# Three sums of weight blocks on GpSimd instead of VectorE, and a new order of the head, in a matmul-tanh-multiply kernel

## The chip, the cores and the metric

The kernel runs on one core of a Trainium2 chip. The metric is the device time of one execution in microseconds, the median of several runs. The engines are named as in the profile: PE (TensorE), DVE (VectorE), ACT (ScalarE), POOL (GpSimd) and SP (SyncE, which only issues DMAs here).

## The reference

```python
x  = randn(16, 512, 1024)   # float32
w1 = randn(1024, 768)
w2 = randn(1024, 768)

def reference(x, w1, w2):
    y1 = np.matmul(x, w1)
    y2 = np.matmul(x, w2)
    return (np.tanh(y1) * y2).astype(np.float32)
```

## The kernel before

The 8192 rows of x are 64 row tiles of 128 ("x rows" below, x0 to x63). Each needs two products with 1024 x 768 weights. The kernel stores w1 and w2 as f16 in one tile `wh`, in rows k0 to k7 of 128 input channels; `u` is w1 and `v` is w2, so u3 is row k3 of w1. It multiplies with f16 on PE and sums in PSUM.

The first four x rows (the head) are done plainly: for each, the chains a (w1, columns 0 to 511), b (w2, the same columns) and G (the last 256 columns of both), of 8 matmuls of 512 columns each (`mm`, L522). The b chain of x3 is kept for the end. The other 60 x rows are done in 20 triples, each with a scheme of fewer multiplications than plain blocks need: 15 block products instead of 18. Each product (`product`, L550) is four matmuls of 512 columns and multiplies a sum of x blocks (`x_sum`, L507, tile `s`) with a sum of w blocks (`w_sum`, L497, tile `b`). The sums are numbered as bit masks: for w, bits 0, 1, 2 are the blocks a, b, G of k0 to k3 and bits 3, 4, 5 those of k4 to k7. So b24 = block 8 + block 16 needs u4 to u7 and v4 to v7; b26 = block 2 - b24; b45 = b37 - block 8. Eleven sums of w blocks, 128 x 2048 f16 each, are made once, on DVE (`B_SUMS`), and then used in all 20 triples. The products that use the three sums above are p1 (s3 with b24), p12 (s35 with b26) and p4 (s10 with b45); b24 also goes into b29 and this into b27, which p0 uses. Ten sums of x blocks are made for each triple (`A_SUMS`), on DVE too, which besides adds partial results (`c_add`, L560) and multiplies with tanh (L529 in the head, L567 in the triples). ACT does tanh, copies out of PSUM and half of the casts of loaded f32 rows to f16 (L427; DVE's casts are L429).

The rows u, v and x0 to x3 are loaded as f32 by the queues of SP and ACT in the order of `SP_LOADS` and `ACT_LOADS` (`y` is an x row). x rows from x4 on are loaded by POOL's queue, in f16 (`load_x`, L471); the first of them (x4 to x6) are transposed on PE like the head's (L463), the later ones by DMA from SP's queue (L474). POOL does no other work but small copies of one column (`gate_x`, L586), which make a load wait until an earlier transpose has landed.

The order of the instructions on each engine is made while the program is built: `Planner.run` gives every operation a duration, a due time and the operations that it needs, and places them. The due times of the head's matmuls are set by `PE_HEAD` (an entry `1a0` is the first half of the a chain of x1, an entry `p7` a product of the first triple) and `HEAD_START`, those of others backwards from their users with `MARGIN`. On the chip there is no clock: each engine takes its instructions in this order, and each waits for the semaphores of what it needs. While data is late PE multiplies constants (`WARM`, and `FILLERS` at named places; L857).

Of the kernel before, what the change touches and what calls it, by code (L numbers as in the profile page):

```python
# [75 lines left out]

PE_HEAD = ("1a0 0a1 1b1 0b1 1G1 p7 p1 0a0 3a0 2b1 p6 0G0 2a1 1b0 1G0 3a1 "
           "p10 3G1 0b0 p9 p12 2G1 p8 1a1 p11 p14 2b0 0G1 3G0 2G0 2a0")  # L80
HEAD_START = 2.5

PE_LAST = "p10 p7 p6 p13- p0- p12 p9 p11 p4- p5- p8 p0 p1 p3- p4 p5 p13 p2- p3 p14 p2 h0 h1"
MUL_DUE = 0.022
MARGIN = {"S": 0.407, "B": 0.262, "T": 5.87, "L": 9.71, "early": 0.060}


WARM = (512, 512, 256)  # L90
FILLERS = {"PT1.0": (512,), "m1b2": (192,), "m1b7": (256,), "PT2.1": (448,)}

EARLY_LOADS = {0: 0.2}
SP_LOADS = ("y0 y1 v7 u3 y2 u1 v4 u0 v0 "
            "v1 v3 u2 u4 v5 v6 u6 u5 u7")
ACT_LOADS = "y3 v2"
POOL_LOADS = "5.0:v5 4.0 4.1 5.1 6"  # L100


class Planner:
# [15 lines left out]
    def op(self, name, engines, due, needs, fn, *args, behind=(), issued=(), chains=(), dma=None, seeds=False, slack=0.0, soon=None):  # L119

        assert name not in self.ops, name
        self.ops[name] = dict(engines=engines, due=due, needs=[n for n in needs if n], behind=[n for n in behind if n],
                              issued=[n for n in issued if n], fn=fn, args=args, chains=chains, dma=dma, seeds=seeds, slack=slack, soon=soon)
        for c in chains:
            self.chains.setdefault(c, {"left": 0, "bank": None})["left"] += 1
# [197 lines left out]
    def spare(self, n):  # L325

        t = self.start_of[n]
        return [b for b in range(len(self.held)) if all(t <= a or z <= t - 1.0 for a, z in self.held[b])][0]


@with_exitstack
def kernel(
# [9 lines left out]
    B, M, K = x.shape  # L342
# [4 lines left out]
    F = 512  # L347
# [9 lines left out]
    PACE, STORES, ST_HEAD, ST3G = "4544", (1.56, 2.37, 3.04), (12, 17, 19), 100  # L357
    sp_loads = ["L" + n for n in SP_LOADS.split()]
    act_loads = ["L" + n for n in ACT_LOADS.split()]
    XF_BUFS, XG_BUFS = 3, max((SP_LOADS + ACT_LOADS).count("y"), 1)  # L360
    ISSUE_SP, ISSUE_ACT, TABLE = 0.495, 0.52, 1.28
# [9 lines left out]
    pool = lambda name, bufs, **k: fast.enter_context(tc.tile_pool(name=name, bufs=bufs, **k))  # L371
# [6 lines left out]
    banks = [pspool.tile([P, F], f32, name=f"bank{i}") for i in range(8)]  # L378
# [24 lines left out]
    plan = Planner(8)  # L403
    op = plan.op
# [189 lines left out]
    DVE_F, DVE_G, DVE_S, DVE_B, DVE_W = (0.60, 0.69), (0.33, 0.42), (0.34, 0.42), (1.23, 1.27), (0.47, 0.56)  # L594
# [3 lines left out]

    head = PE_HEAD.split()
    head_at = {entry: HEAD_START + n * SLOT for n, entry in enumerate(head)}  # L600
    ORIGIN = HEAD_START + (len(head) - 15) * SLOT
    sequence, slot_of = [], {}
# [15 lines left out]
    at, held_at = END - len(tail) * SLOT, {}  # L618
# [8 lines left out]
    parts, early, last, back = {}, set(), "", []  # L627
    both = sorted([(ISSUE_ACT * z, "act", z, n) for z, n in enumerate(act_loads)] + [(ISSUE_SP * z, "sp", z, n) for z, n in enumerate(sp_loads)])
    issuer, last_on = {}, {"act": "", "sp": ""}
    for _, e, z, n in both:  # L630
# [14 lines left out]
        elif n[1] == "x":  # L645
            z = n[2:]
# [19 lines left out]
    last, xh_order, on_pe = "", [], {}  # L666
    for entry in POOL_LOADS.split():
        z, _, gated = entry.partition(":")
        mt, h = (int(v) for v in (z + ".-1").split(".")[:2])
        lo, n = (0, KO) if h < 0 else (h * KH, KH)  # L670
# [29 lines left out]
    for c in "aGb":  # L700
        for mt in range(HEAD):
# [9 lines left out]
            xt_readers[mt] += last  # L711
            due = max(head_at[f"{mt}{c}{h}"] for h in range(2)) + MUL_DUE
            if c == "a":
# [10 lines left out]
    def casts(v):  # L724
        bit = v.bit_length() - 1
        ks = range(bit // 3 * KH, (bit // 3 + 1) * KH)
        return [f"c{c}{k}" for c in ("u", "v", "uv")[bit % 3] for k in ks]

    def w_needs(v):
        return [f"B{v}"] if v in wsum else casts(v)  # L730

    for v, a, b, how in B_SUMS:
        op(f"B{v}", {"dve": DVE_B}, None, w_needs(a) + w_needs(b), w_sum, v, a, b, how)

    def x_needs(i, v):
        if v & (v - 1):
# [24 lines left out]
    for i in range(TRIPLES):  # L761
        until = {}
# [3 lines left out]
    for i in range(TRIPLES):  # L766
# [6 lines left out]
        for o in C_OPS:  # L773
# [19 lines left out]
            if kind in ("t", "th"):  # L793
                lo, n = (0, F) if kind == "t" else (F, G)
                op(f"{name}.{i}", {"act": ACT_F if n == F else ACT_G}, due, needs, c_tanh, i, r, o[4], lo, n, o[5],
                   behind=reuse_out(mt), chains=chains)
            else:
                lo, n, at = (0, F, 0) if kind == "m" else (F, G, G)
# [50 lines left out]

    plan.backward(lambda n: MARGIN["early"] if n in early else MARGIN.get(n[0], 0.2))  # L850
    order = plan.run()
# [3 lines left out]
    def constants(b, n):  # L855

        pin(nc.tensor.matmul(b[:, :n], ones, ones[:, :1].to_broadcast([P, n]), start=True, stop=True))  # L857

    for z, n in enumerate(WARM):
        constants(banks[z], n)  # L860
    first = sp_loads[:2]
# [4 lines left out]
    for n in order:  # L866
        if n not in first:
            o = plan.ops[n]
            for z in FILLERS.get(n, ()):
                constants(banks[plan.spare(n)], z)  # L870
            o["fn"](plan.engine_of[n], *o["args"])
    fast.close()

# [106 lines left out]
```

## Time and profile before

| | |
|---|---|
| median of 3 runs | 298.87 us (298.63 to 299.97) |
| span of the profiled execution | 297.3 us |
| DMA | 64.55 MB, mean 217 GB/s |
| PE clock granted | full in all slices |

A profile row names the source line, the engine, the operation, the tiles written and read, and the shapes. In the rows in order of time the first two numbers are the start and the length in us, counted from the start of the span; "xN" merges N equal instructions that follow each other, and the brackets give the idle time before and what ended it. In the rows of groups the numbers behind the bar are busy us and the mean ns of one instruction. In the chain of waits each row is a piece of the chain that ended last.

### The profile page before, as it was taken

Reading aid. Unit: us, or ns where it says so; the run is one execution under the profiler, and the core shown is the slowest. Engines: PE = TensorE matmul, PEld = TensorE weight load, DVE = VectorE, ACT = ScalarE, POOL = GpSimd, SP = SyncE. Lnnn points to the kernel's source line nnn. Section 1 sums busy time; section 2 is a strip of 40 time slices with the busy share of each in tenths; the row PEclk is TensorE's granted clock in tenths of the full one; section 3 lists DMA queues with packets and bytes.
Section 4 is the critical chain, followed back from the end, with each engine's and each line's share of the span. In section 5 each row is a group of like instructions: output and inputs, shape, how many; then the busy total and the mean of one; then the engine's idle time right before and its main releaser. Section 6 shows DMA issues by size and latency. Waiting matters only on the chain.

```text
span 297.3 us, 4698 instructions
## 1 busy us (share of the span) xinstructions
PE 290.9 (98%) x1419; PEld 137.7 (46%) x1419; DVE 255.5 (86%) x517; ACT 227.6 (77%) x450; POOL 46.7 (16%) x122
## 2 busy tenths in 40 slices
PE   6999999999999999999999999999999999999995
PEld 3545444444444675444444444444444444444443
DVE  1458999999988999898899988989899898999685
ACT  3798988996969769697876979788696866867561
POOL 1024040211030111113121010212101030000000
PEclk9999999999999999999999999999999999999999
DMA  7999999999999999999999999999989899681316
GB/s 263 406 403 230 162 169 222 242 251 258 110 317 212 221 255 244 221 215 259 161 227 217 172 223 199 246 224 215 226 169 245 164 279 244 144 240 47 119 55 215
DMA packets 82827, 64.55 MB, mean 217 GB/s; under 512 B 62704, under 2 KB 64752, under 8 KB 82800
## 3 DMA queue, kind: packets, MB, share of 16 engines
q1 hardware_dynamic: 73584, 47.59, 62.6%
q0 software_dynamic: 8928, 15.73, 34.3%
q10 hardware_dynamic: 288, 0.92, 0.8%
q8 instruction: 11, 0.18, 0.3%
q14 instruction: 16, 0.13, 0.1%
HBM read 39.85 MB, written 25.17 MB: 219 GB/s over the span
## 4 chain that ended last, share of the span: by engine, by line
PE 91%; DMA 6%; ACT 1%; SPq 0%; DVE 0%; issue 0%
PE bank L550 87%; DMA w_f<-in_w_dram 4%; PE bank L522 3%; DMA x_f<-in_x_dram 2%; ACT wh L427 1%; PE bank L463 1%; SPq L423 0%; DVE o_last L529 0%; SPq L415 0%; PE bank L580 0%
## 5 line engine op out<-in xcount | busy, mean ns | idle before, releaser
L550 PE MATMUL bank<-b,s 128*128 128x512 f16 (+1 forms) x664 | 148.1, 371 | 0.0
L550 PEld LDWEIGHTS <-s 128*128 128x128 f16 x832 | 81.2, 98 | 91.4 <-DVE s L507 0.6
L553 ACT ACTIVATE s<-bank 128x512 f32<-128x512 f32 x100 | 58.6, 595 | 41.0 <-PE bank L550 40.5
L560 DVE TENSOR_TENSOR bank<-bank,s 128x512 f32<-128x512 f32 x100 | 69.5, 697 | 18.1 <-PE bank L550 7.8
L477 ACT ACTIVATE junk<-xh 128x1024 f16<-128x1024 f16 x64 | 67.3, 1051 | 0.2
L567 DVE TENSOR_TENSOR o<-o,bank 128x512 f32<-128x512 f32 (+1 forms) x120 | 63.1, 548 | 2.5 <-ACT o L563 1.7
L550 PEld LDWEIGHTS <-xT 128*128 128x128 f16 x412 | 40.3, 98 | 46.1 <-ACT xT L427 0.2
L550 PE MATMUL bank<-b,xT 128*128 128x512 f16 (+1 forms) x252 | 58.5, 369 | 0.0
L563 ACT ACTIVATE o<-bank 128x256 f32<-128x256 f32 (+1 forms) x80 | 33.0, 432 | 12.4 <-PE bank L550 6.1
L550 PE MATMUL bank<-wh,s 128*128 128x512 f16 (+1 forms) x168 | 41.1, 369 | 0.0
L550 PE MATMUL bank<-wh,xT 128*128 128x512 f16 x160 | 40.9, 379 | 0.0
L586 POOL COPY held_x<-xT 128x1 f16<-128x1 f16 x52 | 12.2, 235 | 165.1 <-DMA xT<-xh 165.0
L471 POOL DMA_DIRECT2D xh<-in_x_dram x62 | 33.3, 540 | 20.3 <-issue 6.6
L507 DVE TENSOR_TENSOR s<-s,xT 128x512 f16<-128x512 f16 x80 | 32.3, 421 | 1.2
L563 ACT ACTIVATE o<-s 128x512 f32<-128x512 f32 x40 | 24.9, 623 | 1.2 <-DVE s L560 1.2
L507 DVE TENSOR_TENSOR s<-xT 128x512 f16<-128x512 f16 x60 | 25.0, 418 | 0.0
L553 ACT ACTIVATE bank<-bank 128x512 f32<-128x512 f32 x40 | 21.7, 573 | 1.6 <-DVE bank L560 0.9
L522 PE MATMUL bank<-wh,xT 128*128 128x512 f16 x72 | 18.8, 378 | 0.3
L507 DVE TENSOR_TENSOR s<-xT,s 128x512 f16<-128x512 f16 x40 | 16.7, 417 | 0.0
L560 DVE TENSOR_TENSOR bank<-s,bank 128x512 f32<-128x512 f32 x20 | 13.9, 694 | 1.6
L560 DVE TENSOR_TENSOR s<-s,bank 128x512 f32<-128x512 f32 x20 | 13.6, 681 | 0.3 <-ACT s L553 0.3
L477 ACT ACTIVATE junk<-wh 128x768 f16<-128x768 f16 x16 | 13.5, 842 | 0.2
(42 smaller groups left out, 120.6 us busy)
## 6 DMA issues: line engine op xcount, KB each, us to landing
out_dram<-o SPq DMA_DIRECT2D x54, 384.0 KB, 4.7
xh<-in_x_dram POOLq DMA_DIRECT2D x58, 256.0 KB, 5.7
w_f<-in_w_dram SPq DMA_DIRECT2D x15, 384.0 KB, 6.3
out_dram<-o SPq DMA_DIRECT2D x9, 256.0 KB, 2.0
x_f<-in_x_dram SPq DMA_DIRECT2D x3, 512.0 KB, 4.7
out_dram<-o SPq DMA_DIRECT2D x9, 128.0 KB, 1.7
xT<-xh SPq DMA_TRANSPOSE x57, 5.3
x_f<-in_x_dram ACTq DMA_DIRECT2D x1, 512.0 KB, 4.9
```

Of the source, the lines that this page charges most:

```text
L427: pin(nc.scalar.copy(dst, src))
L463: pin(nc.tensor.transpose(b[:, (k - lo) * P:(k - lo + 1) * P], xhs[mt][:, k * P:(k + 1) * P], ident_h))
L471: pin(nc.gpsimd.dma_start(xhs[mt][:, lo * P:(lo + n) * P], xf[mt][:, lo * P:(lo + n) * P]))
L477: pin(nc.scalar.activation(junk[:, :src.shape[-1]], src, ACT.Abs, scale=scale, accum_out=sums[:, column:column + 1]))
L507: pin(engine[e].tensor_tensor(ss[i, v], x_operand(i, a), x_operand(i, b), OP[how]))
L522: pin(nc.tensor.matmul(shaped(bank(chain)[:, lo:lo + n], w), xts[mt][:, k, :], w, start=begun[chain] == 1, stop=begun[chain] == KO, skip_g ...
L550: pin(nc.tensor.matmul(to, x_operand(i, a)[:, k, :], w, start=begins and k == 0, stop=k == KH - 1, skip_group_check=True))
L553: pin(nc.scalar.activation(place(i, dst, True), place(i, src), ACT.Copy, scale=float(sign)))
L560: pin(nc.vector.tensor_tensor(d, a, b, ALU.add if signs == (1, 1) else ALU.subtract))
L563: pin(nc.scalar.activation(out_tile(HEAD + 3 * i + r)[:, lo:lo + n], place(i, src)[:, :n], ACT.Tanh, scale=float(sign)))
L567: pin(nc.vector.tensor_tensor(o, o, place(i, src)[:, at:at + n], ALU.mult))
L586: pin(nc.gpsimd.tensor_copy(held_x, xts[mt][:, 0, :1]))
```

## The change

Three of the eleven sums of w blocks, b26, b45 and b24, are made on POOL (`POOL_B`). All the tables that set the order of the head are replaced: `PE_HEAD`, `HEAD_START`, `MUL_DUE`, `MARGIN`, the orders of loads for the three queues, and the list of fillers, which is now worked out from the planner's own gaps (`fillers`).

```diff
-PE_HEAD = ("1a0 0a1 1b1 0b1 1G1 p7 p1 0a0 3a0 2b1 p6 0G0 2a1 1b0 1G0 3a1 "
-           "p10 3G1 0b0 p9 p12 2G1 p8 1a1 p11 p14 2b0 0G1 3G0 2G0 2a0")
-HEAD_START = 2.5
+PE_HEAD = ("0a1 0b1 p1 3a0 2a1 1a0 3G1 1G1 3G0 0G1 1a1 0G0 p7 p6 2b1 p10 p9 0a0 1b0 p12 1G0 0b0 2G1 "
+           "2b0 3a1 p8 p11 p14 2a0 1b1 2G0")
+HEAD_START = 4.535
-MUL_DUE = 0.022
-MARGIN = {"S": 0.407, "B": 0.262, "T": 5.87, "L": 9.71, "early": 0.060}
+MUL_DUE = -1.445
+MARGIN = {"S": 0.773, "B": 0.02, "T": 3.425, "L": 8.221, "early": 0.01}
-FILLERS = {"PT1.0": (512,), "m1b2": (192,), "m1b7": (256,), "PT2.1": (448,)}
-SP_LOADS = ("y0 y1 v7 u3 y2 u1 v4 u0 v0 "
-            "v1 v3 u2 u4 v5 v6 u6 u5 u7")
-ACT_LOADS = "y3 v2"
-POOL_LOADS = "5.0:v5 4.0 4.1 5.1 6"
+SP_LOADS = "y0 v4 y1 u3 u4 v0 u1 v7 v1 u2 v3 v5 u6 u7 u5 v6"
+ACT_LOADS = "y2 y3 u0 v2"
+POOL_B = (26, 45, 24)
+POOL_LOADS = "5.0:v5 6 5.1 4.0 4.1"
...
+    def fillers(self, until):
+
+        found, busy = {}, None
+        for n in sorted((n for n in self.ops if self.engine_of[n] == "pe"), key=lambda n: self.start_of[n]):
+            t = self.start_of[n]
+            if t > until:
+                break
+            if busy is not None and t - busy > 0.32 and self.spare(n):
+                found[n] = self.spare(n)[0], int((t - busy - 0.12) * 600) // 32 * 32
+            busy = t + self.ops[n]["engines"]["pe"][0]
+        return found
...
-        op(f"B{v}", {"dve": DVE_B}, None, w_needs(a) + w_needs(b), w_sum, v, a, b, how)
+        op(f"B{v}", {"pool": (4.6, 4.7)} if v in POOL_B else {"dve": DVE_B}, None, w_needs(a) + w_needs(b), w_sum, v, a, b, how)
...
+    fillers = plan.fillers(24.0)
...
-            for z in FILLERS.get(n, ()):
-                constants(banks[plan.spare(n)], z)
+            if n in fillers:
+                b, z = fillers[n]
+                for at in range(0, z, F):
+                    constants(banks[b], min(F, z - at))
```

What this does to the order of the built program is seen at three places. The source lines of the change are 11 higher (w_sum is L508, x_sum L518, load_x L482), 14 at the end.

On POOL, behind the copy that starts the x loads (`held`). `xh` with a number is an x row; before, the sums are not there:

```order
L589 COPY held_88<-w_f_227 128x1
L471 DMA xh_277<-in_x_dram 128x512
L471 DMA xh_282<-in_x_dram 128x512 x2
L471 DMA xh_277<-in_x_dram 128x512
L471 DMA xh_296<-in_x_dram 128x1024
L471 DMA xh_301<-in_x_dram 128x1024
L471 DMA xh_305<-in_x_dram 128x1024
L471 DMA xh_312<-in_x_dram 128x1024
L471 DMA xh_318<-in_x_dram 128x1024
L471 DMA xh_425<-in_x_dram 128x1024
```

And with the change:

```order
L482 DMA xh_300<-in_x_dram 128x1024
L482 DMA xh_304<-in_x_dram 128x1024
L482 DMA xh_311<-in_x_dram 128x1024
L508 TENSOR_TENSOR b24_101<-wh_95 128x2048
L482 DMA xh_383<-in_x_dram 128x1024
L508 TENSOR_TENSOR b26_106<-wh_95,b24_101 128x2048
L482 DMA xh_447<-in_x_dram 128x1024
L508 TENSOR_TENSOR b45_102<-b37_100,wh_95 128x2048
L597 COPY held_x_89<-xT_404 128x1
L482 DMA xh_497<-in_x_dram 128x1024
```

The sums stand between the loads of x9 to x12, which wait for them on POOL's queue.

On DVE, from the cast of the last w row that DVE casts (`w_f_256` is u7, in the change `w_f_258` is v6) to the first sums of x. Before:

```order
L429 CAST wh_95<-w_f_256 128x768
L497 TENSOR_TENSOR b24_101<-wh_95 128x2048
L497 TENSOR_TENSOR b36_98<-wh_95 128x2048
L529 TENSOR_TENSOR o_333<-o_333,bank7_84 128x512
L497 TENSOR_TENSOR b37_100<-wh_95,b36_98 128x2048
L507 TENSOR_TENSOR s3_379<-xT_341 128x512
L507 TENSOR_TENSOR s10_382<-xT_341,xT_366 128x512
L507 TENSOR_TENSOR s11_390<-s3_379,xT_366 128x512
L507 TENSOR_TENSOR s15_394<-s11_390,xT_366 128x512
```

With the change:

```order
L440 CAST wh_95<-w_f_258 128x768
L508 TENSOR_TENSOR b36_98<-wh_95 128x2048
L540 TENSOR_TENSOR o_last_323<-o_last_323,bank2_79 128x256
L508 TENSOR_TENSOR b37_100<-wh_95,b36_98 128x2048
L540 TENSOR_TENSOR o_326<-o_326,bank4_81 128x512
L540 TENSOR_TENSOR o_331<-o_331,bank5_82 128x512
L440 COPY xT_369<-bank4_81 128x512
L440 COPY xT_355<-bank2_79 128x512
L508 TENSOR_TENSOR b18_103<-wh_95 128x2048
L518 TENSOR_TENSOR s3_399<-xT_369 128x512
L540 TENSOR_TENSOR o_326<-o_326,bank3_80 128x256
L518 TENSOR_TENSOR s11_411<-s3_399,xT_355 128x512
```

b24 is gone from this place; two products and two copies out of PSUM (banks) and the sum b18 stand ahead of s3, the sum that the first product p1 reads.

On SP, the loads at the start (`x_f` is an x row in f32, `w_f` a row of w). Before:

```order
L415 DMA x_f_120<-in_x_dram 128x1024
L415 DMA x_f_122<-in_x_dram 128x1024
L423 DMA w_f_133<-in_w2_dram 128x768
L423 DMA w_f_135<-in_w1_dram 128x768
L415 DMA x_f_137<-in_x_dram 128x1024
L423 DMA w_f_153<-in_w1_dram 128x768
```

With the change:

```order
L426 DMA x_f_120<-in_x_dram 128x1024
L434 DMA w_f_122<-in_w2_dram 128x768
L426 DMA x_f_133<-in_x_dram 128x1024
L434 DMA w_f_137<-in_w1_dram 128x768
L434 DMA w_f_147<-in_w1_dram 128x768
L434 DMA w_f_168<-in_w2_dram 128x768
```

SP now loads two of the first four x rows instead of three, and ACT's queue the other two.

More of the change, by code (lines that the diff above doesn't have):

```diff
@@ L327, in spare @@
         t = self.start_of[n]
-        return [b for b in range(len(self.held)) if all(t <= a or z <= t - 1.0 for a, z in self.held[b])][0]
+        return [b for b in range(len(self.held)) if all(t <= a or z <= t - 1.0 for a, z in self.held[b])]
+    def fillers(self, until):
[8 more added lines that the diff above has]
+        return found
 @with_exitstack
```

## The prediction

> **What bounds the kernel now.** I read the page first, then the chain that ended last, then TensorE's (PE's) own rows in the head, and then, because the change gives GpSimd (POOL) arithmetic, every place where a POOL instruction met a VectorE (DVE) one.
>
> ```profile
> span 297.3 us, 4698 instructions
> PE 290.9 (98%) x1419; PEld 137.7 (46%) x1419; DVE 255.5 (86%) x517; ACT 227.6 (77%) x450; POOL 46.7 (16%) x122
> PE   6999999999999999999999999999999999999995
> DVE  1458999999988999898899988989899898999685
> ```
>
> PE is the bound: every slice but the first and last is full. DVE is next, and full from the fifth to the eleventh slice (30 to 82 us); the moved sums lie just before that stretch and in it. The chain in order of time says where PE's time can still shrink:
>
> ```profile
> 16.13 5.95 DMA w_f<-in_w_dram
> 22.10 0.84 ACT wh L427
> 22.98 3.40 PE bank L522 x15
> ...
> 36.63 242.78 PE bank L550 x1168
> ```
>
> Up to 22.98 us PE waits for loads of w (through a cast); behind it the chain stays on PE. So an order can gain only in the head, and anything that makes PE wait behind 23 us is added to the end in full.
>
> ```profile
> 6.80 1.07 PE L463 MATMUL bank<-ident_h,xh 128*128 128x128 f16 x16 [1.59 <-ACT xh L427]
> ...
> 8.70 0.62 PE L463 MATMUL bank<-ident_h,xh 128*128 128x128 f16 x8
> 9.16 0.38 PE L522 MATMUL bank<-wh,xT 128*128 128x512 f16 x1
> 9.38 0.49 PE L857 MATMUL bank<-ones 128*128 128x192 f32 x2
> ...
> 10.00 0.60 PE L857 MATMUL bank<-ones 128*128 128x256 f32 x2
> ...
> 11.57 0.92 PE L857 MATMUL bank<-ones 128*128 128x448 f32 x2
> 12.45 0.62 PE L463 MATMUL bank<-ident_h,xh 128*128 128x128 f16 x8
> ...
> 21.62 1.74 PE L522 MATMUL bank<-wh,xT 128*128 128x512 f16 x6
> ```
>
> The L857 rows are fillers, multiplied for nothing while data is late. Sixteen transposes against eight (1.07 - 0.62 = 0.45 us for 8) make one transpose 0.056 us.
>
> ```profile
> 31.00 1.03 PE L550 MATMUL bank<-wh,xT 128*128 128x512 f16 x4
> 31.86 1.89 PE L550 MATMUL bank<-b,s 128*128 128x512 f16 x8
> ```
>
> Eight products against four: 0.86 / 4 = 0.215 us each. From 9.16 to 22.98 (13.82 us) the L522 rows count 49 plain products and one group of 8 transposes: 10.5 + 0.45 us of work, so about 2.8 us of fillers and waits. That bounds what a new order of loads can win there.
>
> **The change part by part: the head.** The loads of w set the pace. Casts on DVE that wait for them:
>
> ```profile
> 5.89 0.69 DVE L429 CAST xh<-x_f 128x1024 f16<-128x1024 f32 x1 [4.65 <-DMA x_f<-in_x_dram]
> ...
> 17.22 0.56 DVE L429 CAST wh<-w_f 128x768 f16<-128x768 f32 x1 [3.51 <-DMA w_f<-in_w_dram]
> 18.19 0.56 DVE L429 CAST wh<-w_f 128x768 f16<-128x768 f32 x1 [0.41 <-DMA w_f<-in_w_dram]
> ...
> 24.12 0.56 DVE L429 CAST wh<-w_f 128x768 f16<-128x768 f32 x1 [0.90 <-DMA w_f<-in_w_dram]
> ```
>
> One w row (384 KB) lands every 0.97 us, the last at 24.1; a row of x (512 KB) then takes 1.3 us. The change loads the same bytes, so its last w row (v6) also lands at about 24.1. What moves is who comes first. Now all four x rows and v4 and u0 come ahead. The first two x rows land by 5.9 us (DVE's first cast starts then in the trace, 5.89); v4, two x rows and u0 are 1792 KB more, 4.5 us at 0.97 us for 384 KB, so the fourth x lands at about 10.4. Its cast (0.69 us on DVE) and 8 transposes end at about 11.7 us, and till then PE has done only two plain products, against seven in the old order (the row at 12.45 is the next transposes). From there PE goes load by load: u0 with four x rows and v4 with one (5 products) to 12.8; u3 lands at 12.3 and is cast on ScalarE (ACT) in 0.84 us, a wait of 0.4; v2, u4, v0, u1, v7, v1, u2, v3 and v5 feed 3 to 5 products each, about 1.0 us of work for 0.97 us of load, without a wait; u6 and u7, both cast on ACT, cost 0.3 and 0.1. At 23.0 us this gives 50 plain products, one more than before: 0.2 us. Behind 23 us the old order loses 0.16 us more, in a hole ahead of these transposes (three products are 0.65 us, and 0.81 pass):
>
> ```profile
> 25.57 0.81 PE L522 MATMUL bank<-wh,xT 128*128 128x512 f16 x3
> 26.38 0.40 PE L463 MATMUL bank<-ident_h,xh 128*128 128x128 f16 x4
> ```
>
> I take a gain of **0.4 us** for the new head. The bounds: if the fourth x comes 0.9 us earlier, which is as much as sharing the queues otherwise can give, the gain is 1.3 us; if u3, u6 and u7 each come half a load later, it is a loss of 0.7 us.
>
> What DVE saves, three sums of 1.22 us, is worth nothing to PE: PE did not wait for DVE once behind 23 us (the chain from 36.63 on is PE's own for 242.78 us).
>
> **The change part by part: the three sums on POOL.** What they compete for is seen where POOL's small copies (one column, L586) meet DVE. Beside a DVE instruction that reads a PSUM bank:
>
> ```profile
> 57.49 0.70 DVE L560 TENSOR_TENSOR bank<-bank,s 128x512 f32<-128x512 f32 x1
> ```
> ```profile
> 57.71 0.19 POOL L586 COPY held_x<-xT 128x1 f16<-128x1 f16 x1 [3.26 <-DMA xT<-xh]
> ```
>
> The copy takes 0.19 us, undisturbed. Beside a sum of w blocks, whose inputs both lie in SBUF:
>
> ```profile
> 42.11 1.22 DVE L497 TENSOR_TENSOR b<-b,wh 128x2048 f16<-128x2048 f16 x1
> ```
> ```profile
> 42.34 1.03 POOL L586 COPY held_x<-xT 128x1 f16<-128x1 f16 x1 [0.53 <-DMA xT<-xh]
> ```
>
> Here it takes 1.03 us and ends at 43.37, just behind the sum's end at 43.33. And between two sums that stand back to back on DVE:
>
> ```profile
> 87.89 0.42 DVE L507 TENSOR_TENSOR s<-xT,s 128x512 f16<-128x512 f16 x1
> 88.23 0.88 DVE L507 TENSOR_TENSOR s<-s,xT 128x512 f16<-128x512 f16 x2
> ```
> ```profile
> 88.03 0.33 POOL L586 COPY held_x<-xT 128x1 f16<-128x1 f16 x1 [1.19 <-DMA xT<-xh]
> ```
>
> It ends at 88.36, behind the first sum's end (88.31), although DVE's next sum was already queued. So a DVE sum out of SBUF and a POOL instruction out of SBUF do not run together; the one that is first is finished; and POOL, waiting, gets in ahead of DVE's next. If this holds the other way round, a long POOL sum stops DVE at its first sum out of SBUF, and DVE being in order, everything behind that too. The Trainium skill (SBUF — State Buffer, "Who interferes with whom") states exactly this: a DVE instruction with two SBUF inputs and a GpSimd instruction that reads SBUF contend for one read interface, and whoever issues first holds it for the whole instruction; the three rows agree for DVE first, and no row here shows POOL first.
>
> How long is a POOL sum, D? No row has one.
>
> ```profile
> L586 POOL COPY held_x<-xT 128x1 f16<-128x1 f16 x52 | 12.2, 235 | 165.1 <-DMA xT<-xh 165.0
> L865 POOL CAST ident_h<-ident 128x128 f16<-128x128 f32 x1 | 0.3, 294 | 0.1
> ```
>
> One column undisturbed 0.19, 128 columns 0.29: 0.8 ns a column for one input. For 2048 columns that is 1.8 us if the second input is free, 3.4 us if it costs as much as the first, 5.0 us if reading twice and writing each cost a slope. I take **D = 3.4** (two inputs, two reads) and keep 1.8 and 5.0. The Trainium skill (GPSIMD Engine Reference, 3.1) gives 4.5 us for a two-input sum of 2048 fp32 elements; by that figure the sum below would end 3.3 us later, at about 309.5.
>
> When they run: b24 needs the last cast, v6 (24.1 + 0.6 = 24.7), and POOL's eight issues of x loads ahead of it:
>
> ```profile
> 20.69 4.65 POOL L471 DMA_DIRECT2D xh<-in_x_dram  x8
> ```
> ```profile
> 24.78 2.36 DVE L497 TENSOR_TENSOR b<-wh 128x2048 f16<-128x2048 f16 x2
> ```
>
> They end at 25.3. On DVE the sums that need the last cast begin at 24.78; b36 is now the first of them and runs 1.22 us, to 26.0. The queue from there, by the order of the built program, with the durations of these rows:
>
> ```profile
> L497 DVE TENSOR_TENSOR b<-wh 128x2048 f16<-128x2048 f16 x6 | 7.2, 1222 | 0.4 <-ACT wh L427 0.2
> L507 DVE TENSOR_TENSOR s<-xT 128x512 f16<-128x512 f16 x60 | 25.0, 418 | 0.0
> L529 DVE TENSOR_TENSOR o<-o,bank 128x512 f32<-128x512 f32 x3 | 2.0, 680 | 0.0
> L429 DVE COPY xT<-bank 128x512 f16<-128x512 f16 x4 | 1.6, 422 | 3.5 <-PE bank L463 3.5
> ```
>
> - b24 gets in at 26.0, ends 26.0 + D = 29.4. DVE does the product into o_last (PSUM input) and stops at b37.
> - b37 29.4 to 30.6. POOL issues one x load (0.55) and then waits; it gets in behind b37: b26 30.6 to 34.0.
> - DVE does two products out of PSUM (0.7 each) and two copies out of PSUM (0.4 each), stops at b18, which runs 34.0 to 35.2.
> - POOL issues another load and waits; it gets in ahead of s3: b45 35.2 to 38.6.
> - s3 38.6 to 39.0; the first product of the steady part, p1, which needs b24 and s3, starts at 39.1.
>
> Undisturbed, PE would reach p1 at 23.0 + 22 plain products (4.7) + 24 transposes (1.3) + 11 plain products (2.4) = 31.4 us, and s3 would be there: b36, b37 and b18, four products and copies, and s3 itself end at about 31.4. So p1 is 39.1 - 31.4 = **7.7 us** late. In between PE also stops for a bank: the transposes of the first half of x row 4 (xh_291) go into bank 4, which the product behind b37 frees at 31.3, where PE would want it at 28.6; these 2.7 us are part of the 7.7. Once b45 is done, DVE has s11, s15, s31, s34, s35 ahead of it at 0.34 each while PE takes 0.86 for each product, so I count nothing behind it. The x loads that POOL issues between its sums are late with them, the third triple's two or so by about 3 us, but PE reaches the third triple only some 26 us (two triples of 15 products of 0.86) behind p1. On SP the store of o_last now stands ahead of the first transposes of x; its product ends at 26.4 on DVE, ahead of the first transpose's start:
>
> ```profile
> 30.15 10.81 SPq L474 DMA_TRANSPOSE xT<-xh  x5
> ```
>
> So these two cost nothing. The plain form is p1 = 28.9 + 3D: D = 1.8 gives a shift of 2.9, 5.0 one of 12.5.
>
> Sum on the profiled execution: 297.3 - 0.4 + 7.7 = 304.6 us; the median lies 1.57 us above the span (298.87), which gives **306.2 us**. The bounds are 301.4 (D = 1.8) and 311.0 (D = 5.0).
>
> **The rivals.**
> 1. *They run side by side* (POOL does not stop DVE). For it: no row shows a POOL instruction holding DVE, and the copies are too short to show it. Then b24 ends at 25.3 + 3.4 = 28.7, b26 at 32.7, b45 at 36.7, against needs at 31.4 (p1), 36.1 (p12, 22 matmuls behind p1) and 44.5 (p4, 61 behind): all hidden, and only the head's 0.4 us is left: 298.5 us, not slower. It decides below D = 0.9 too.
> 2. *POOL gives way* (it stands whenever DVE sums, without holding DVE). Then b24 takes D plus the DVE sums in its way, b37, b18 and the rest of b36: 3.4 + 3.1 = 6.5 us, to 31.8; b26 follows at 32.4 with some 2.7 us of s sums in its way, to 38.5, where PE wants it at 36.1: 2.4 us late, 300.9 us. For it: the row at 42.34. Against: the row at 88.03, where POOL went ahead of a queued DVE sum.
> 3. *The head gains more than I see*, its full 1.3 us and 0.2 us of holes too short to see here, with the sums hidden: 297.4 us. Against: loads end at 24.1 either way, and 38 plain products, 8.2 us, and p1 stand behind that in both orders.
>
> That the sums are not moved at all is excluded by the built order.
>
> **How the numbers follow.** Forecast (POOL holds DVE) 0.56, rival 2 0.14, rival 1 0.22, rival 3 0.08. About 0.5% (1.5 us) is what a measurement here can tell from no change. The forecast and rival 2 (2.0 us over) are slower: 0.70; rival 1 is the same: 0.22; rival 3 lies at that bound: faster 0.08. The forecast's own range is 301.4 to 311.0; the range that also takes in the rivals from 298.0 up, and D up to 4.8, is 298.0 to 310.5.
>
> **What would show it.** Right: POOL rows of some 3 us and more for three sums, each starting as a DVE sum ends; DVE rows of sums (b37, b18, and s3 or the next) that last or wait as long as a POOL sum; PE idle between 28 and 40 us, waiting for DVE. Wrong: DVE sums of 0.42 and 1.22 us beside a running POOL sum (rival 1); POOL rows of 6 us and DVE undisturbed (rival 2). My head is wrong if PE has not 50 plain products done at 23 us. The forecast fails as a whole if POOL takes the interface piece by piece, or if D is under 1 us.

## The result, and the profile after

The changed kernel took 309.47 us (median of four runs, 308.75 to 310.44) against 299.16 us for the kernel before on the same chip: a ratio of 1.0345, 95% interval [1.0316, 1.0373], 10.3 us slower. The forecast was 306.2 us in a range of 298.0 to 310.5, slower at 0.70. The profiled execution took 310.44 us with a span of 308.9; the span before was 297.3, so 11.6 us are to be found. The profiled executions of two runs below, those of the fourth x row and of POOL only writing, were 6.9 and 3.6 us longer than their medians; PE lost that time behind 50 us, and only rows ahead of it are read from them.

The page of the changed kernel, busy times, PE's slices and the chain's share by engine:

```profile
PE 295.3 (96%) x1419; PEld 138.7 (45%) x1419; DVE 260.7 (84%) x518; ACT 226.3 (73%) x446; POOL 58.7 (19%) x125
PE   7799659999999999999999999999999999999995
PEclk9999789999999999999999999999999999999999
PE 86%; DMA 6%; DVE 4%; issue 2%; ACT 1%; DVEq 0%
```

DVE lost three sums, took two casts and two copies over from ACT, and is busy 5.2 us longer. The lost time lies in slices 5 and 6 (31 to 46 us): PE is at 6 and 5 tenths there, and the granted clock, full before, is at 7 and 8 tenths. From slice 7 on everything is as it was. POOL's rows of the changed kernel in that stretch (start, length, both in us):

```profile
27.78 4.10 POOL L508 TENSOR_TENSOR b<-wh 128x2048 f16<-128x2048 f16 x1
31.81 0.57 POOL L482 DMA_DIRECT2D xh<-in_x_dram  x1
32.40 4.49 POOL L508 TENSOR_TENSOR b<-wh,b 128x2048 f16<-128x2048 f16 x1
37.95 0.57 POOL L482 DMA_DIRECT2D xh<-in_x_dram  x1 [1.06 <-ACT junk L488]
38.55 4.07 POOL L508 TENSOR_TENSOR b<-b,wh 128x2048 f16<-128x2048 f16 x1
```

And DVE's:

```profile
26.71 1.22 DVE L508 TENSOR_TENSOR b<-wh 128x2048 f16<-128x2048 f16 x1
28.06 0.42 DVE L540 TENSOR_TENSOR o_last<-o_last,bank 128x256 f32<-128x256 f32 x1
28.40 4.57 DVE L508 TENSOR_TENSOR b<-wh,b 128x2048 f16<-128x2048 f16 x1
32.90 1.27 DVE L540 TENSOR_TENSOR o<-o,bank 128x512 f32<-128x512 f32 x2
34.10 0.92 DVE L440 COPY xT<-bank 128x512 f16<-128x512 f16 x2
34.94 3.03 DVE L508 TENSOR_TENSOR b<-wh 128x2048 f16<-128x2048 f16 x1
37.90 0.41 DVE L518 TENSOR_TENSOR s<-xT 128x512 f16<-128x512 f16 x1
38.23 0.41 DVE L540 TENSOR_TENSOR o<-o,bank 128x256 f32<-128x256 f32 x1
38.56 4.81 DVE L518 TENSOR_TENSOR s<-s,xT 128x512 f16<-128x512 f16 x2
```

The two tables are to be read against each other. b36 (26.71) runs its 1.22 us undisturbed. b37 starts at 28.40, 0.62 us behind POOL's b24, and ends at 32.97, 1.1 us behind the end of b24 (31.88): it ran only then. b18 (34.94) ends 1.1 us behind the end of b26 (36.89), s11 (38.56) behind the end of b45 (42.62). A held instruction is shown as a long one, not as idle time. What reads a PSUM bank (28.06, the first 0.42 us beside b24) is not held. PE's rows:

```profile
30.25 0.84 PE L474 MATMUL bank<-ident_h,xh 128*128 128x128 f16 x12 [0.32 <-DMA xh<-in_x_dram]
...
33.62 0.87 PE L474 MATMUL bank<-ident_h,xh 128*128 128x128 f16 x8 [2.32 <-DVE o L540]
...
35.14 3.14 PE L533 MATMUL bank<-wh,xT 128*128 128x512 f16 x9
38.37 1.04 PE L561 MATMUL bank<-b,s 128*128 128x512 f16 x4
39.24 1.03 PE L561 MATMUL bank<-wh,xT 128*128 128x512 f16 x4
43.43 1.32 PE L561 MATMUL bank<-b,s 128*128 128x512 f16 x4 [3.17 <-DVE s L518]
```

The wait at 33.62 is the one for bank 4, whose product stands on DVE behind b37. The wait at 43.43 is product p6's for s15, behind s11. And nine plain products, 2.1 us at 0.215 each, take 3.14 from 35.14. The clock says why (a window, its length, PE's, PEld's, DVE's, ACT's and POOL's busy time, then the granted clock):

```profile
34.00:36.00 2.00, 2.00 (x13) 1.17 (x12) 1.93 (x4) 0.58 (x1) 2.00 (x1) 0.50 1.36 202
36.00:38.00 2.00, 2.00 (x8) 0.74 (x6) 2.00 (x2) 1.73 (x4) 0.94 (x2) 0.69 1.01 132
38.00:44.00 6.00, 2.75 (x13) 1.01 (x12) 5.93 (x6) 4.38 (x9) 5.98 (x6) 1.00 1.11 169
44.00:46.00 2.00, 2.00 (x7) 0.76 (x5) 1.93 (x5) 0.00 (x0) 1.06 (x3) 0.51 0.81 135
```

Behind each of the two waits PE ran at half clock for 3.4 us, and then at full clock again.

The account, made by taking for each matmul of the work its start less the work done ahead of it at full clock, in the traces of before and after: PE is 2.15 us later than before when it reaches the transposes at 30.25; the wait for bank 4 adds 2.5, the half clock behind it 1.9, the wait for s15 3.3, the half clock behind that 1.7. Together 11.6 us, and behind 48 us no more than 0.2 us comes to it.

### The profile page after: what moved, and what is told of

Read it like the earlier page. It is cut to its first block, busy times and chain, and to the rows that moved or that the text cites. A ratio compares the mean times of both kernels' runs of the same rounds, so it can differ in the third digit from the quotient of the medians.

```text
span 308.9 us, 4697 instructions
## 1 busy us (share of the span) xinstructions
PE 295.3 (96%) x1419; PEld 138.7 (45%) x1419; DVE 260.7 (84%) x518; ACT 226.3 (73%) x446; POOL 58.7 (19%) x125
## 4 chain that ended last, share of the span: by engine, by line
PE 86%; DMA 6%; DVE 4%; issue 2%; ACT 1%; DVEq 0%
PE bank L561 84%; DMA x_f<-in_x_dram 3%; DMA w_f<-in_w_dram 2%; PE bank L533 2%; DVE s L518 2%; DVE b L508 1%; ACT wh L438 1%; DVE o L540 1%; DVE xh L440 0%; DVE o_last L540 0%; ACT xT L438 0%; DVE xT L440 0%; PE bank L474 0%; ACT o_last L536 0%; ACT o L536 0%
## 5 line engine op out<-in xcount | busy, mean ns | idle before, releaser
L564 ACT ACTIVATE s<-bank 128x512 f32<-128x512 f32 x100 | 59.2, 595 | 40.2 <-PE bank L561 39.2
L597 POOL COPY held_x<-xT 128x1 f16<-128x1 f16 x52 | 11.2, 215 | 167.2 <-DMA xT<-xh 166.9
L561 PE MATMUL bank<-wh,xT 128*128 128x512 f16 x160 | 41.8, 385 | 0.0
L482 POOL DMA_DIRECT2D xh<-in_x_dram x62 | 33.3, 539 | 16.4 <-issue 8.5
L518 DVE TENSOR_TENSOR s<-s,xT 128x512 f16<-128x512 f16 x80 | 36.0, 466 | 0.2
L518 DVE TENSOR_TENSOR s<-xT 128x512 f16<-128x512 f16 x60 | 23.9, 416 | 0.0
L533 PE MATMUL bank<-wh,xT 128*128 128x512 f16 x72 | 21.3, 406 | 0.6 <-DVE wh L440 0.3
L518 DVE TENSOR_TENSOR s<-xT,s 128x512 f16<-128x512 f16 x40 | 16.7, 417 | 0.0
```

Source lines behind the costliest of these rows:

```text
L482: pin(nc.gpsimd.dma_start(xhs[mt][:, lo * P:(lo + n) * P], xf[mt][:, lo * P:(lo + n) * P]))
L518: pin(engine[e].tensor_tensor(ss[i, v], x_operand(i, a), x_operand(i, b), OP[how]))
L533: pin(nc.tensor.matmul(shaped(bank(chain)[:, lo:lo + n], w), xts[mt][:, k, :], w, start=begun[chain] == 1, stop=begun[chain] == KO, skip_g ...
L561: pin(nc.tensor.matmul(to, x_operand(i, a)[:, k, :], w, start=begins and k == 0, stop=k == KH - 1, skip_group_check=True))
L564: pin(nc.scalar.activation(place(i, dst, True), place(i, src), ACT.Copy, scale=float(sign)))
L597: pin(nc.gpsimd.tensor_copy(held_x, xts[mt][:, 0, :1]))
```

## The experiments

Two theories went in: the prediction's (POOL's sums hold DVE's, one after another; the new order is worth little), and against it that the new order itself, its head or its placing of DVE's sums, makes the loss. Ratios are to runs of the kernel before on the same chip.

**POOL's sums cut to 16 columns, in the new order.**

```diff
+        if e == "pool":
+            blocks = [z.rearrange("p k (t n) -> p k t n", t=2) if len(z.shape) == 3 else z for z in blocks]
+            blocks = [z[:, 0, 0, :16] for z in blocks]
...
+    for v in POOL_B:
+        pin(nc.gpsimd.memset(wsum[v], 0.0))
```

> The changed kernel with its three sums on POOL cut to 16 columns (the rest of b24, b26 and b45 is set to 0 by three POOL memsets at the start, so most of these sums is left out); the order of all engines else is that of the change. Theory (a POOL sum holds DVE's sums out of SBUF for its whole length): the waits of PE at 31 to 34 and at 40 to 43 us vanish, the granted clock stays full, and only the later head is left, a PE deficit of 10.78 to 12.93, so 2.1 us over the kernel before: 300.5 to 302.0 us. Rival A (the new order of DVE and the banks costs it, not the POOL sums): 306 us or more.

301.19 us, ratio 1.0075 [1.0051, 1.0099], as the theory has it. The long sums carry most of the loss. Up to 1.1 us of what is left may be the experiment's own: its memsets on POOL at the start made the first cast on DVE take 1.81 us, where it took 0.69 before.

```profile
5.88 1.81 DVE L440 CAST xh<-x_f 128x1024 f16<-128x1024 f32 x1 [4.63 <-DMA x_f<-in_x_dram]
```

**The kernel before with only the three sums moved, its old order kept.**

```diff
-        op(f"B{v}", {"dve": DVE_B}, None, ...
+        op(f"B{v}", {"pool": (4.6, 4.7)} if v in (26, 45, 24) else {"dve": DVE_B}, None, ...
```

> The kernel before with only the three sums given to POOL, its own orders of loads and head kept. Theory: three holds of about 4 us on a DVE that is full there, so PE waits 5 to 9 us: 303 to 309 us. Rival A (it is the new order): 298.5 to 300 us.

309.96 us, ratio 1.0379 [1.0345, 1.0413]: the whole loss, without the new order, and 1.0 us above the theory's range. POOL's sums took 4.59, 4.47 and 4.07 us, and DVE's rows show the three holds:

```profile
26.01 4.96 DVE L497 TENSOR_TENSOR b<-wh,b 128x2048 f16<-128x2048 f16 x1
...
32.09 3.09 DVE L507 TENSOR_TENSOR s<-xT 128x512 f16<-128x512 f16 x1
...
35.62 4.82 DVE L507 TENSOR_TENSOR s<-xT 128x512 f16<-128x512 f16 x1
```

**The new order with all eleven sums on DVE** (`POOL_B = ()`).

> The changed kernel with all eleven sums on DVE (the planner places them anew), new tables kept. Theory: no hold, only the later head: 300.5 to 302.0 us. Rival A: 306 us or more. My own forecast of the head (0.4 us gained) would give 298.7 us.

303.12 us, ratio 1.0135 [1.0102, 1.0169], 1.1 us above the theory's range: PE was 12.2 us behind its work at 29.5 us (10.8 before), and the sums, back on DVE, came too late for some products between 38 and 52 us:

```profile
PE bank L561 <- DVE s L571: 1.0, 1, 1.0
PE bank L561 <- DVE b L508: 0.6, 1, 0.6
```

So the order is no gain by itself: in this execution it cost 1.4 us in the head, and where all sums are DVE's some 3 us behind it, 1.6 of them in these two waits.

**The change, with the fourth x row loaded into a tile that is still free (that of b48).** In the changed kernel this load was issued only at 6.69 us, since x rows have three buffers, and landed at 12.48, not at the predicted 10.4.

```diff
-            x32[mt] = xfpool.tile([P, K], f32, tag="xf", name="x_f")
+            x32[mt] = wsum[48].rearrange("p k f -> p (k f)").bitcast(f32) if mt == 1 else xfpool.tile(...)
```

> The changed kernel, but the load of the fourth x row of the head gets a buffer of its own (the place of b48, which is made only near 50 us), so that it no longer waits at 6.7 us for the first cast; same order. Theory (the head is late because this load starts late, its cast then holds back the cast of u0 on DVE, and w buffers come free late): the last w row lands near 24.1 us instead of 26.0 and the time falls by 1.5 to 2.2 us against the change, to 307.3 to 308.0. Rival B (the order of the loads as such is the cause): no change, 309.2 to 309.8.

309.75 us, ratio 1.0338 [1.0312, 1.0365]: no change, the rival's number and not the theory's. In the profiled execution the row landed at 10.57 and the last w row at 24.50 instead of 26.02, but the seven traces of this order of loads without the edit have the last row anywhere from 24.12 to 26.31, so it is not shown that the edit brought it forward. PE then waited longer at p1:

```profile
40.70 1.89 PE L561 MATMUL bank<-b,s 128*128 128x512 f16 x4 [5.62 <-POOL held_x L597]
```

(POOL's copy stands there by name only; s3 ended just then, behind b45.) b45 got in ahead of s3 here, so p1 waited for all three holds, and what the earlier row gained went into that wait: the two plain products behind p6 start at 46.21, in the change at 46.24.

**The same with all sums on DVE.**

> The new order with all eleven sums on VectorE, and the fourth x row loaded into a tile that is not yet used (that of b48), so that its load waits for no buffer. Without that edit the same kernel took 303.1 us, and PE was then 12.2 us behind at 29.5 us and lost 3 us more to late sums between 38 and 52 us. Theory (the head lost its time by the fourth x row's wait for a buffer, and the holds of POOL's sums alone gave the gain back in the run with POOL): the last w row lands at about 24.5 instead of 26.0, and with no POOL sum that is kept: PE is 1.5 us earlier at 30 us, and the time is 299.5 to 301.8. Rival (the late x row is not what sets the head): no change, 302.5 to 303.5.

301.90 us, ratio 1.0083 [1.0058, 1.0108], 0.1 us above the theory's range. Without holds the earlier row seems to be worth 1.5 us (1.0135 to 1.0083, but the two intervals touch). In the profiled execution the last w row landed late all the same, 2.5 us behind the one before it, so where a gain comes from is not shown.

**POOL busy as long, but only writing.**

```diff
+        if e == "pool":
+            for _ in range(2):
+                pin(engine[e].memset(wsum[v], 0.0))
+            return
```

> The change, with each of POOL's three sums replaced by two memsets of the same tile of 128x2048: POOL is busy at the same places for 2 x 1.80 = 3.6 us each, but reads nothing. The three sums are left out. Theory (what holds DVE is reading SBUF from two sides): DVE's sums b37, b18 and s3 run at 1.22 and 0.42 us beside POOL's memsets, PE has no wait for DVE over 1 us between 30 and 44 us, and the time is that with the sums cut short, 301.2, within 300.5 to 302.5 (b26 still waits for b37 and p12 for b26, which leaves room for up to 1 us). Rival (any long POOL instruction holds DVE, reading or not): DVE instructions of 3 to 5 us and 306.5 to 309.5.

300.78 us, ratio 1.0043 [1.0013, 1.0072], within the theory's range. POOL's and DVE's rows of this kernel:

```profile
25.78 3.69 POOL L510 MEMSET b<- 128x2048 f16 x2
...
29.94 3.69 POOL L510 MEMSET b<- 128x2048 f16 x2
```
```profile
25.78 1.23 DVE L512 TENSOR_TENSOR b<-wh 128x2048 f16<-128x2048 f16 x1
...
27.25 1.22 DVE L512 TENSOR_TENSOR b<-wh,b 128x2048 f16<-128x2048 f16 x1
...
31.04 1.22 DVE L512 TENSOR_TENSOR b<-wh 128x2048 f16<-128x2048 f16 x1
32.17 0.42 DVE L522 TENSOR_TENSOR s<-xT 128x512 f16<-128x512 f16 x1
```

Beside 3.69 us of writing on POOL, b37, b18 and s3 take their own 1.22 and 0.42 us. What holds DVE is POOL's reading of SBUF, not its being busy. The price of the holds, the half clock behind them included, is then 1.0345 - 1.0043, 3.0% or 9.0 us (the two intervals allow 2.4 to 3.6%), and that of the new order with DVE left alone and the three sums left out 1.3 us. With all sums on DVE the same tables cost 1.0135, so in the new order taking three sums off DVE is worth some 0.9%, if nothing holds it (the planner also places the sums anew there). The Trainium skill (SBUF — State Buffer, "Who interferes with whom") has it so too: two-input DVE sums contend with what reads on GpSimd and not with what only writes, while a cast can run in a mode that takes the whole shared pair of ports, for reading and writing. The sums here and the 1.81 us cast above agree.

**Constants on PE in the two pauses of the change**, two of 512 columns ahead of x row 4's transposes and five ahead of p6.

> The change, with constants multiplied on PE in the two places where it stood idle for 2.3 and 3.2 us: ahead of the transposes of the first half of x row 4 and ahead of the first triple's product p6. Theory (PE ran at half clock for some 3.6 us behind each of these pauses because it had paused, and the clock cost 1.9 us, most of which was again wait for DVE, and 1.7 us): the granted clock stays full from 30 us on; the pauses stay as waits; the time falls by 1.5 to 2.1 us, to 307.4 to 308.0. Rival A (the half clock has another cause): no change, 309.2 to 309.8. Rival B (the fillers stand in the way themselves, since they are not over when DVE is): 309.8 or more.

314.61 us, ratio 1.0502 [1.0448, 1.0557]: the theory's range is missed by far, and rival B has it. In the first pause the theory held: the clock stayed full to 39.2 us. But in this execution the last w row landed at 24.47, and b45 got in ahead of s3, as the prediction had it. The first POOL sum, and PE's rows from p1 on:

```profile
26.23 4.09 POOL L509 TENSOR_TENSOR b<-wh 128x2048 f16<-128x2048 f16 x1
```
```profile
40.66 1.89 PE L562 MATMUL bank<-b,s 128*128 128x512 f16 x4 [5.61 <-POOL held_x L598]
42.34 1.91 PE L562 MATMUL bank<-wh,xT 128*128 128x512 f16 x4
44.05 5.47 PE L869 MATMUL bank<-ones 128*128 128x512 f32 x10
49.37 1.02 PE L562 MATMUL bank<-b,s 128*128 128x512 f16 x4
```

The pause was now ahead of p1 and not of p6. The five constants stood behind it, where no data were missing, and took 5.47 us, the first 2.0 of them at half clock: pure loss.

**Each POOL sum in four pieces of 512 columns.**

```diff
+        if e == "pool":
+            for k in range(KH):
+                pin(engine[e].tensor_tensor(*[z[:, k] for z in blocks], OP[how]))
+            return
```

> The change, with each of POOL's three sums made in four instructions of 512 columns instead of one of 2048. Theory (POOL holds the read of SBUF for one instruction at a time, and DVE gets in between): POOL pieces of 1.0 to 1.2 us, no DVE sum lasts more than its own time and 1.2 us, s3 and b18 come some 3 us earlier, and the time is 302 to 307. Rival (POOL keeps DVE out from the first piece to the last, since its next piece is queued when one ends): no change, 309 to 310.

311.45 us, ratio 1.0389 [1.0333, 1.0444]: no gain, and 1.5 us above even the rival's range. The pieces of b24 took 1.12 us each (4.48 for four), and DVE's b36, already waiting, came in between none of them:

```profile
25.49 6.52 DVE L512 TENSOR_TENSOR b<-wh 128x2048 f16<-128x2048 f16 x1
```
```profile
26.05 4.48 POOL L510 TENSOR_TENSOR b<-wh 128x512 f16<-128x512 f16 x4
```

DVE's turn came when POOL turned to a load, at 30.47 us. s15 waited in the same way through all four pieces of b45 (39.45 to 44.59 us). In b26 it went otherwise: b37 came in between the first piece and the second, which took 2.12 us with this wait in it.

```profile
31.05 6.27 POOL L510 TENSOR_TENSOR b<-wh,b 128x512 f16<-128x512 f16 x4
```
```profile
32.26 1.84 DVE L512 TENSOR_TENSOR b<-wh,b 128x2048 f16<-128x2048 f16 x1
```

So a queued POOL instruction can get in ahead of a waiting DVE sum piece after piece, but does not always; what decides it is not shown, nor why b36, which shows from 25.49, had not begun when the first piece did at 26.05.

**POOL makes half of each sum.**

```diff
+        if e == "pool":
+            blocks = [z[:, :KH // 2] for z in blocks]
...
+    for v in POOL_B:
+        pin(nc.vector.memset(wsum[v][:, KH // 2:], 0.0))
```

> The change with POOL making only the first half (1024 columns) of each of its three sums; the other half is left out (zeroed at the start on DVE, which is idle then). A POOL sum should take 2.0 to 2.3 us. Theory (each POOL sum holds DVE for its whole length, three in series): p1's time is 28.9 + 3D as the prediction has it, so 2.1 us less of D takes 6.3 us off, less what the half clock adds or not: between the change at 309.5 and the order with undisturbed DVE at 300.8, at 302 to 305. Rival (the price is one of the handover, not of the length, so that each POOL sum costs about the same): 306.5 or more. Rival B (the half is short enough to be hidden): 301.3 or less.

305.73 us, ratio 1.0218 [1.0195, 1.0240], between the ranges: 0.7 us above the theory's and 0.8 below the rival's. The price falls with the length, but not in proportion: over the run that only writes it is 1.75% for half sums and 3.0% for whole ones. Half sums took 2.14 to 2.18 us. Since b24's half reads only rows k4 and k5, it did not wait for the last row and held the cast of that row (4.02 us, of which the first 1.4 lie ahead of the half sum, beside POOL's issues); PE paused 2.96 us for the cast and ran at half clock behind it, which the estimate did not have:

```profile
25.02 4.02 DVE L440 CAST wh<-w_f 128x768 f16<-128x768 f32 x1 [1.80 <-DMA w_f<-in_w_dram]
29.14 3.27 DVE L510 TENSOR_TENSOR b<-wh 128x2048 f16<-128x2048 f16 x1
```

**The kernel before with b45 alone on POOL.**

> The kernel before with b45 alone on POOL, the sum that is wanted last of the three (by p4, and on DVE at 42.1 us in the trace of before). It starts when b37 is there (28.8 us) and holds DVE for some 4.1 us at s3 or s10, so that s3 comes at up to 33.0 instead of 29.2 and p1, at 31.9 us on PE, is 1.2 to 2.2 us late. Theory: 300.5 to 302.3, a wait of PE for DVE between 31 and 35 us. Rival (one sum is hidden by the slack of DVE, which gets 1.22 us back at 42 us): 298.7 to 300.0.

302.54 us, ratio 1.0114 [1.0092, 1.0136], 0.24 us above the theory's range. One hold, two waits of PE (2.64 and 0.79 us), no half clock:

```profile
28.85 4.62 DVE L507 TENSOR_TENSOR s<-xT 128x512 f16<-128x512 f16 x2
```
```profile
34.71 1.89 PE L550 MATMUL bank<-b,s 128*128 128x512 f16 x8 [2.64 <-DVE o L529]
```

Even the sum that is wanted last costs 3 us.

**Six constants ahead of p1, in the old order with the three sums on POOL.**

> The kernel before with the three sums on POOL (310.0 us), and six constants of 512 columns multiplied on PE ahead of product p1, into p6's bank, which is free by then. In the run without them PE stood idle there for 5.9 us and then ran at half the granted clock from 41.2 to some 44 us, losing 1.75 us more. Six such products took 5.2 us (0.87 each) where they ran at full clock, so they are over before p1's sums are there. Theory (the clock is halved because PE stood idle): the wait for p1 is hidden behind the constants, the granted clock is full from 35 to 48 us, and the time falls by 1.4 to 1.9 us, to 308.0 to 308.7. Rival (the half clock has another cause, or the constants end after p1's data are there): 309.7 or more.

309.88 us, ratio 1.0359 [1.0337, 1.0381], against 1.0379 without them: no gain, and the rival's range. The wait for p1 was covered and the clock was full behind it (38 to 48 us), as expected. But now the clock was halved behind the first pause, which had the same length (3.27 us, and 3.26 without the constants, where the clock stayed full), so PE reached the constants some 1.6 us later and was busy with them to 41.95 us, while p1's bank, which a product behind the held sum on DVE frees, was free at 41.04. Windows of the run with the constants, and behind them one of the run without:

```profile
32.00:34.00 2.00, 2.00 (x15) 1.15 (x12) 2.00 (x2) 1.58 (x3) 2.00 (x1) 0.68 1.44 159
...
38.00:48.00 10.00, 9.71 (x36) 4.15 (x35) 9.93 (x16) 3.01 (x7) 4.99 (x7) 1.00 0.92 128
```
```profile
31.00:34.00 3.00, 2.38 (x20) 1.45 (x20) 3.00 (x3) 1.83 (x3) 3.00 (x1) 1.00 1.08 173
```

That the clock fell because PE paused is borne out (where the pause was filled, it stayed full, twice); that filling pays is not shown, in either order.

No run points to a version below the kernel before.

## Why the prediction was right, and where not

**POOL holds DVE: right, and shown.** Three holds one after another, each to the end of a POOL sum, with DVE in order behind it (the run with the old order has all of the loss, the run that only writes 1.3 us of it). The wait for bank 4 was foreseen too, with 2.7 us against 2.32. POOL, waiting, gets in ahead of DVE's next sum: right where it came to that (b45 ahead of s3 in two traces), but no rule, as b37 between the pieces shows.

**D = 3.4: too small.** The whole sums took 4.07 to 4.60 us in all runs, the longest of them with a wait for DVE inside; undisturbed 4.1. Of the bounds 1.8 and 5.0, taken from one-column and 128-column copies, the value lay in the upper half. The Trainium skill (GPSIMD Engine Reference, 3.1) gives 4.5 us for fp32, nearer than the slope of the rows; the f16 sums here took 4.07 to 4.10 undisturbed. That a D of 4.5 would have brought the prediction's sum to 309.5, the measured time, is luck: with 4.1 the sum gives 308.3, and the rest came from terms that it had at nothing or with the wrong sign.

**The queue: right in some executions, and the form with it.** Where the last w row landed early (the run with the fourth x row, the run with constants), b45 stood ahead of s3, and p1 came at 40.70 and 40.66 us. The prediction's p1 = 28.9 + 3D gives 40.7 for the 3.94 us by which b24 kept DVE in the latter (from the end of b36 at 26.38 to 30.32). That it fits so closely is partly luck: b36 ended 0.38 us later than forecast, and the steps between the holds took as much less. In the profiled execution of the change itself, POOL's load ahead of b45 waited 1.06 us for ACT, s3 got in first, and p1 came at 38.37.

**"I count nothing behind it" failed.** With s3 through, b45 held s11 and s15 instead, and p6 waited 3.17 us. It makes nearly the same sum in another place: at 50 us PE was 11.4 us later than before in this trace, and 10.8 in that of the fourth x row, where b45 stood ahead of s3 (medians 309.47 and 309.75 us).

**The clock was not in the sum.** Half clock behind the two pauses cost 1.9 and 1.7 us. The first lies ahead of a wait that DVE ends, so that only the second adds to the end.

**The head: wrong in sign.** The step "the fourth x lands at about 10.4, the last w row at about 24.1" failed. The load waited for one of three x buffers (issued at 6.69), landed at 12.48 with another row that shared the time, its cast stood on DVE ahead of u0's, and w buffers came free late; the last cast started at 26.05 against 24.12 before. The prediction's own test, 50 plain products done at 23 us, failed with 43. In place of a gain of 0.4 us there was a loss of 2.15 in this execution; the run that only writes puts the new order at 1.3 us, that with short sums at 2.2. The six other traces of the same order of loads have the fourth x row at 11.4 to 12.4 us, 41 to 48 plain products at 23 us, and the last w row at 24.1 to 25.0 in five and at 26.3 in one. So the late fourth x row and the loss belong to the order, part of the 2.15 to this execution, and what delays the last row in some executions stays open.

**The sum.** The profiled execution is 11.55 us longer where 7.3 was forecast (7.7 - 0.4), 4.25 us more (the median lies 1 us below that execution). DVE's queue ends the last wait, so read it there: p6 stood at 40.8 in the forecast (39.1 and two products of 0.86) and started at 43.43, 2.6 us later. 1.9 of these are the late last w row (b36 ended at 27.93 where 26.0 was forecast, and the holds began with that); the rest, some 0.7, is D, 0.5 to 0.7 larger three times (1.75 together), less the 1.1 us that s15 had in hand against p6 in the forecast. The other 1.7 us are the half clock behind p6. The lateness of PE itself ahead of p6, by the head and by the first half clock, is covered by this wait.

**What DVE saves is worth nothing to PE: not borne out.** It was read from the order of before, for which no run tests it; in the new order the run that only writes, with three sums less on DVE, stands at 1.0043 against 1.0135 with all on DVE. That the x loads on POOL's queue would not matter: right, no wait for a load is left behind 31 us.

## What to carry to other kernels

Before an operation goes to POOL to relieve DVE, look at what stands on DVE during it: with both reading SBUF they take turns by whole instructions, and a 1.22 us sum that becomes a 4.1 us sum elsewhere can cost DVE up to 4.1 us. One copy of 1.03 instead of 0.19 us beside a DVE sum told this in the trace of before. Cutting the POOL work in pieces gave DVE a turn in one of three sums here, and no time; filling a pause helps only where its place is fixed.

## What the runs showed of the hardware beside this

- The granted clock halves behind a pause of PE, but the pause's length does not settle it: pauses of 2.32, 2.96, 3.17, 3.27 and over 5 us did it, pauses of 1.75, 2.64 and 3.26 us did not, and the 3.26 and 3.27 us are the same place of the same order. What settles it is where the pause lies. Each trace records when the granted clock changes, and in all 13 traces these times are whole multiples of 3.41 us apart (in the change: down at 33.81, up at 37.23, down at 44.05, up at 47.47). This grid, laid through each trace from its first full clock, cuts it into windows of 3.41 us. Every window at full clock in which PE was idle for 2.06 us or more was followed by half clock (the 2.06 at the end of a program, the next 2.32), and every one with 1.88 us or less by full clock:

| pause, run | its idle time in the windows that it touches | clock in the next |
|---|---|---|
| 2.32 us, the change, ahead of x row 4's transposes | 2.32 | half |
| 3.27 us, old order with constants | 0.94, 2.33 | half, behind the second |
| 3.26 us, old order without them | 1.80, 1.46 | full |
| 2.64 us, b45 alone on POOL | 1.05, 1.59 | full |

- Half clock lasted one such window, 3.4 us, or two, 6.8 us, as in the run with constants (39.2 to 46.1 us). The Trainium skill (TensorE: Matmul & The Clock Gate, "What's actually happening") has a free-running window of some 3.4 us, and the traces agree. It has the clock fall after an idle window; here 2.06 us of idle time in one were enough.
- A cast from f32 to f16 on DVE can be held by more than a sum is: 1.81 us beside POOL's memset (0.69 alone), and 1.53 and 0.93 instead of 0.56 us beside POOL's issuing of x loads in two traces, though in the change and four other traces the same cast took its 0.56 us beside such issues. The row of the 1.53 us:

```profile
24.14 1.53 DVE L440 CAST wh<-w_f 128x768 f16<-128x768 f32 x1 [1.83 <-DMA w_f<-in_w_dram]
```

- The same program's loads do not land alike: v2, the sixth load, landed at 12.3 us in the profiled execution of the change and between 10.1 and 10.8 in the six others with the same order of loads.
